# Block products in the mixer's input projections, kept weight sums, paused modulation rows and a reordered start, on an 8-core decoder trunk

## The chip, the cores and the metric

The kernel runs on the eight cores of one Trainium2 chip; each core works on one of eight sequences, with the same weights. The metric is the device time of the slowest core in microseconds (us). Cores 0 to 3 are one die, 4 to 7 the other; I call 0-1, 2-3, 4-5 and 6-7 pairs. Some executions of any kernel fall into a slow state, in which a whole die runs at a lower granted clock; those runs are called slow, and only fast runs are compared unless I say otherwise. The calls for chip time fell on different chips, which are told apart here by their numbers: 8, 14, 4, 10 and 7. The chip of the first measurement is not known.

## The reference, cut to what matters

```python
D_MODEL = 1024; BATCH = 8; SEQ = 2048; DEPTH = 2; D_FF = 2816
# each sub-layer: RMSNorm -> shift/scale from c -> f -> gate -> residual add
# layer 0: SwiGLU, mixer_ab, SwiGLU; layer 1: SwiGLU, mixer_pool, SwiGLU
def mixer_ab(h, w_in, norm_v, w_s, b_s, conv_w, w_out):
    proj = h @ w_in                                # (B, S, 2560)
    u, v, bg, cg, xb = jnp.split(proj, [...], axis=-1)        # 512 columns each
    y_a = spatial_gating(jax.nn.gelu(u), jax.nn.gelu(v), norm_v, w_s, b_s)
    y_b = bg * causal_short_conv(cg * xb, conv_w)
    return jnp.concatenate([y_a, y_b], axis=-1) @ w_out
# mod = silu(c) @ w_mod[l] + b_mod[l]   -> shift, scale and gate of each sub-layer: the "modulation rows"
# ... swiglu, spatial_gating, causal_short_conv, mixer_pool, final RMSNorm
```

The program works in passes of 1,024 tokens, two per sub-layer, each of two tiles of 512 tokens.

## The kernel before

A small list scheduler in the kernel's own code places every instruction on its engine in order of modelled time.

The SwiGLU layers ("FFN" below) already multiply by seven block products in place of eight: a 2 x 2 block matrix product after Strassen and Winograd, with sums of weight blocks and of activation blocks made on DVE, and sums of products made on DVE and ACT. The mixer's input projections u and the three conv sections use plain products:

```python
def u_part(tt, hd):                      # gate u: 8 products per output of 128 x 512
    b = bank(); pc = W["u", hd // 2]; ff = hd % 2
    for c in range(NC):
        mm(PS[b][:], SL[:, pc.slot, (ff * 8 + c) * 128:(ff * 8 + c + 1) * 128], HH.ap(c, tt), c == 0, c == NC - 1, ...)
    act(TP[:, gu, 0:TT], PS[b][:], AF.Gelu_apprx_tanh, ...)
# ... and for the conv sections, three banks at a time:
for si in range(3):
    for c in range(NC):
        mm(PS[b][:], SL[:, pcs[si].slot, ...], HH.ap(c, tt), c == 0, c == NC - 1, ...)
```

Weights lie in six slots in SBUF; a slot is loaded again when its piece has been used up. The modulation rows (144 per core, each a dot product of 131,072 weights with `silu(c)`) are streamed in small portions: sixteen at the start, on which everything waits, and 128 later, one per eight segments of work, wherever the schedule has DVE time:

```python
SLG = (2, 3, 4, 6, 7, 7)     # load of slot s waits for the shift row of chunk SLG[s]
on_pe = (10, 12, 14, 15)     # these four of the first 16 rows are dotted ...
def row0(k):
    for n, q in ((2 * k, c), (2 * k + 1, 8 + c)):
        if n in on_pe:       # ... on PE, by eight products of one column
            for kc in range(NC):
                add("pe", I("matmul", PS[b][:, 0:1], ap[...], CT[:, kc:kc + 1], ...), cost=0.25)
        else:                # DVE: multiply and accumulate, 1.2 us
            stt(ap, ap, 1.0, CB[:], ALU.mult, ALU.mult, ..., accum_out=M)
for s, k in zip(range(NSLOT), SLG):
    load_next(s, [("MOD", 0, order0[k])])
# later rows
def rows_pump():
    row_tick[0] += 1
    if row_tick[0] >= ROW_EVERY and rows_on[0] and slack():
        row_tick[0] -= ROW_EVERY
        # ... take the next row: row_dot(q) on DVE, prefetch another
```

## Time and profile before

| | before |
|---|---|
| median of the first three runs | 1933.72 us (1932.42 to 1934.73) |
| spans of the eight cores in the profiled run | 1921.6 to 1928.1 us |
| PE / DVE / ACT busy | 98% / 88% / 53% |
| f16 products of 512 columns on input projections | 5440 |
| continuous products begin | 67 to 71 us, by core |

A line of the table by stage gives a window, its length, the busy time of each engine with its number of instructions, the granted clock of TensorE as a share of full speed (PEclk), the mean busy share of the 16 DMA engines and their rate. The prediction shows the lines that bound the kernel. One line that it did not look at is the clock row of the page, in tenths of full speed, one digit per fortieth of the span:

```profile
PEclk9899999999999999999999999999999999999999
```

A 9 means 0.9 or more. After the first 100 us the clock is full.

### The profile page before, as it was taken

To read this page: it belongs to the slowest core of one execution; us is meant where nothing else is said; L and a number is where in the kernel's file an instruction comes from. 1 tells how busy PE (TensorE), PEld (TensorE's weight loads), DVE (VectorE), ACT (ScalarE), POOL (GpSimd) and SP (SyncE) were. 2 spreads that over 40 slices of the span, in tenths; PEclk is the share of its full clock that TensorE was granted. 3 is DMA by queue.
4 is the path that set the end of the run, shared out by engine and by line. 5 is a ranking of instruction groups with operands and counts; after the bars stand their busy time and mean duration, and the time that the engine had idled before them with its cause. 6 is when DMAs were issued, how large, how long until landed. Compare 5 with 4: busy or idle time off the path is not lost.

```text
span 1928.1 us, 25440 instructions; the slowest of 8 cores (1921.6 to 1928.1 us)
## 1 busy us (share of the span) xinstructions
PE 1883.1 (98%) x8722; PEld 855.1 (44%) x8722; DVE 1692.6 (88%) x3252; ACT 1030.2 (53%) x1742; POOL 175.9 (9%) x333
## 2 busy tenths in 40 slices
PE   4999999999999999999999999999999999999997
PEld 1544444444444444444444444444444444444443
DVE  4797999999888899999999888888999899998865
ACT  4444854455464564555456554654556655574343
POOL 0000000001112000000000000000000000000000
PEclk9899999999999999999999999999999999999999
DMA  9679658787776676767774554555453545445852
GB/s 277 141 174 220 115 104 188 169 189 152 172 156 153 144 146 160 166 140 151 166 175 80 88 88 85 88 99 87 74 92 66 88 77 97 79 76 85 177 84 92
DMA packets 67661, 248.72 MB, mean 129 GB/s; under 512 B 7632, under 2 KB 7760, under 8 KB 67280
## 3 DMA queue, kind: packets, MB, share of 16 engines
q0 software_dynamic: 42192, 153.64, 47.4%
q1 hardware_dynamic: 25056, 92.67, 15.1%
q8 instruction: 74, 1.21, 0.2%
q10 hardware_dynamic: 288, 0.79, 0.1%
q14 instruction: 51, 0.42, 0.1%
HBM read 392.29 MB, written 8.39 MB: 208 GB/s over the span
## 4 chain that ended last, share of the span: by engine, by line
PE 93%; DMA 4%; SPq 1%; DVE 1%; ACT 0%; issue 0%; POOL 0%
PE ps L480 93%; DMA WMOD<-wmod 3%; SPq L480 1%; DMA SLOTS<-win 1%; DMA ACTB<-wmod 0%; DVE X L480 0%; DVE ACTB L480 0%; DVE WMOD L480 0%; ACT PMH L480 0%; ACT ps L480 0%; ACT ACTB L480 0%; ACT RS L480 0%; ACT L480 0%; DVE TP L480 0%; ACT TP L480 0%
## 5 line engine op out<-in xcount | busy, mean ns | idle before, releaser
L480 PE MATMUL ps<-H,SLOTS 128*128 128x512 f16 x5440 | 1197.4, 379 | 3.1 <-DVE ps L480 1.3
L480 PEld LDWEIGHTS ps<-H,SLOTS 128*128 128x128 f16 x5440 | 531.0, 98 | 648.3 <-issue 14.6
L480 ACT ACTIVATE ps<-ps 128x512 f32<-128x512 f32 x684 | 398.0, 582 | 585.3 <-PE ps L480 577.7
L480 PE MATMUL ps<-ACTB,SLOTS 128*128 128x512 f16 x2780 | 614.2, 379 | 0.8 <-DVE X L480 0.8
L480 PEld LDWEIGHTS ps<-ACTB,SLOTS 128*128 128x128 f16 x2780 | 271.9, 98 | 329.1 <-issue 1.5
L480 DVE TENSOR_TENSOR SLOTS<-SLOTS 128x512 f16<-128x512 f16 x996 | 392.6, 418 | 16.3 <-DMA SLOTS<-win 11.0
L480 DVE SCALAR_TENSOR_TENSOR X<-ps,GH,X 128x512 f32<-128x512 f32 x424 | 307.5, 746 | 34.4 <-PE ps L480 29.4
L480 ACT ACTIVATE TP<-ps 128x512 f32<-128x512 f32 x400 | 237.8, 595 | 124.4 <-PE ps L480 121.9
L480 DVE TENSOR_TENSOR ACTB<-TP,ps 128x512 f16<-128x512 f32 x368 | 248.1, 683 | 33.5 <-PE ps L480 20.9
L480 POOL DMA_DIRECT2D SLOTS<-win x176 | 93.1, 530 | 1039.1 <-PE ps L480 965.3
L480 ACT ACTIVATE SQ<-X 128x512 bf16<-128x512 f32 x224 | 131.0, 622 | 84.2 <-DVE X L480 42.0
L480 DVE TENSOR_TENSOR TP<-ps,TP 128x512 f32<-128x512 f32 x176 | 121.0, 688 | 48.7 <-ACT ps L480 47.6
L480 DVE SCALAR_TENSOR_TENSOR WMOD<-WMOD,CB 128x1024 f32<-128x1024 f32 x130 | 158.0, 1217 | 3.3 <-DMA WMOD<-wmod 3.3
L480 DVE TENSOR_TENSOR ps<-ps,TP 128x512 f32<-128x512 f32 x176 | 122.5, 696 | 13.4 <-PE ps L480 11.4
L480 DVE TENSOR_TENSOR TP<-X,RS 128x512 f32<-128x512 f32 x192 | 127.5, 683 | 6.6 <-ACT ACTB L480 4.8
L480 DVE TENSOR_TENSOR ACTB<-ACTB 128x1024 f16<-128x1024 f16 (+1 forms) x188 | 104.4, 566 | 1.3
L480 POOL DMA_DIRECT2D SLOTS<-wout x88 | 46.5, 528 | 489.4 <-PE ps L480 482.2
L480 PE MATMUL ps<-SQ,ONES 128*128 128x512 bf16 x182 | 59.6, 431 | 28.1 <-ACT SQ L480 25.8
L480 ACT ACTIVATE H<-TP,MODT,AS 128x512 f16<-128x512 f32 x81 | 62.3, 805 | 23.6 <-DVE TP L480 12.0
L480 ACT ACTIVATE PMH<-TP,MODT,AS 128x512 f16<-128x512 f32 x60 | 47.4, 804 | 9.4 <-DVE TP L480 9.3
L480 ACT ACTIVATE ACTB<-TP,MODT,AS 128x512 f16<-128x512 f32 x51 | 40.0, 805 | 13.3 <-PE ps L480 7.1
L480 DVE TENSOR_TENSOR H<-H 128x1024 f16<-128x1024 f16 (+1 forms) x72 | 43.2, 623 | 2.1 <-ACT H L480 2.1
(78 smaller groups left out, 531.5 us busy)
## 6 DMA issues: line engine op xcount, KB each, us to landing
SLOTS<-win POOLq DMA_DIRECT2D x176, 512.0 KB, 5.7
WMOD<-wmod SPq DMA_DIRECT2D x131, 512.0 KB, 5.5
SLOTS<-wout POOLq DMA_DIRECT2D x88, 512.0 KB, 5.4
SLOTS<-wab POOLq DMA_DIRECT2D x28, 512.0 KB, 8.1
outT<-X SPq DMA_DIRECT2D x14, 512.0 KB, 4.5
ACTB<-wmod SPq DMA_DIRECT2D x13, 512.0 KB, 27.9
X<-xT SPq DMA_DIRECT2D x2, 2048.0 KB, 22.0
X<-xT SPq DMA_DIRECT2D x8, 512.0 KB, 9.7
```

The source lines that it names most:

```text
L480: return lambda E: getattr(E, name)(*a, **k)
```

## The change

The intent: seven block products for u and the three conv sections too (64 products fewer in the two passes); the weight block sums of six conv pieces are stored in DRAM by pass one and read by pass two; the normalisation of v moves from DVE to ACT; modulation rows pause in the mixer; and the start is reordered, with one row fewer on PE and the first weight loads later in the queue.

```diff
-SLG = (2, 3, 4, 6, 7, 7)
+SLG = (5, 6, 6, 7, 7, 7)
+AB_KEEP = (4, 5, 6, 7, 8, 9)
@@ sums of the mixer's conv pieces: pass one keeps, pass two reads
+            for n in AB_KEEP:
+                a["w"][AB_PIECES[n]].keep = b["w"][AB_PIECES[n]].kept = n_kept
+                n_kept += 1
@@ rows
-    SLACK = 2.5
+    SLACK = 2
-        rows_on[0] = True
+        rows_on[0] = sub[0] == "F"
+        row_tick[0] = 0
@@ seven products per unit of 256 outputs x 1024 tokens
+    def mix_segments(units):
+        def prod(u, b, wq, hq, first): ...
+        def P1(u): ...
+        # ... P5, P2, P6, P7, P3, P4
+        for w, fs in ((u, (P1, P5)), (v, (P7, P3)), (u, (P2,)), (v, (P4,)), (u, (P6,))): ...
@@ normalisation of v
-            ts(Av4[:, blk, :], TP[:, gv, 0:TT], STAT[:, st, 6:7], STAT[:, st, 9:10], ALU.subtract, ALU.mult, ...)
+            add("pool", I("tensor_scalar", out=STAT[:, st, 10:11], ..., op0=ALU.mult, op1=ALU.mult), ...)
+            act(Av4[:, blk, :], TP[:, gv, 0:TT], AF.Identity, ..., scale=STAT[:, st, 9:10], bias=STAT[:, st, 10:11])
@@ mixer body
-        for tt in range(2):
-            for hd in range(4): u_part(tt, hd) ...
+        for f in mix_segments([u_unit(f) for f in range(2)]): ...
-        for hf in range(2):  # 24 x 8 products
+        for f in mix_segments([mix_unit(sec, hf) for hf in range(2) for sec in (3, 4, 2)]): ...
@@ start
-    on_pe = (10, 12, 14, 15)
+    on_pe = (10, 12, 14)
-                                ..., cost=0.25)
+                                ..., cost=0.43)
```

(The rest of the diff is cut: buffers of the conv chain, the order of pieces, renamed keys.)

## The prediction

> **What bounds the kernel now.** I read the page first, then the chain of waits in order of time, the matmul engine's own waits, a table by stage, the vector engine's groups in the first mixer pass, and the timeline of the start. The page and its chain:
>
> ```profile
> PE 1883.1 (98%) x8722; PEld 855.1 (44%) x8722; DVE 1692.6 (88%) x3252; ACT 1030.2 (53%) x1742; POOL 175.9 (9%) x333
> PE 93%; DMA 4%; SPq 1%; DVE 1%; ACT 0%; issue 0%; POOL 0%
> ```
>
> Busy PE alone proves little, since matmuls are pipelined. What matters is that 93% of the chain is PE following PE, and that PE has almost nothing to wait for after the start; its waits in the whole run, largest first:
>
> ```profile
> PE ps L480 <- ACT SQ L480: 25.8, 3, 18.9
> PE ps L480 <- DVE ps L480: 1.3, 1, 1.3
> PE ps L480 <- DVE X L480: 0.8, 1, 0.8
> ```
>
> The 25.8 us lie in the first 35 us and in the tail. So between about 70 and 1915 us a product removed is a product's time saved, unless another engine takes over. Whether one can is in the table by stage (columns: window and its length, PE, PEld, DVE, ACT, POOL busy with counts, clock, DMA share, GB/s). Rows are the FFN pass before the mixer, the mixer's two passes, the FFN pass after, and two later stretches:
>
> ```profile
> 373.00:474.00 101.00, 101.00 (x469) 45.66 (x468) 98.10 (x190) 58.03 (x97) 9.14 (x17) 1.00 0.80 173
> 474.00:574.00 100.00, 100.00 (x488) 46.30 (x487) 83.76 (x146) 53.98 (x94) 16.02 (x31) 1.00 0.74 168
> 574.00:675.00 101.00, 101.00 (x493) 46.79 (x492) 87.20 (x151) 53.01 (x93) 15.99 (x31) 1.00 0.65 147
> 675.00:775.00 100.00, 100.00 (x465) 45.12 (x463) 96.52 (x195) 50.86 (x87) 8.16 (x16) 1.00 0.71 153
> 1080.00:1180.00 100.00, 100.00 (x465) 45.28 (x463) 79.81 (x152) 50.00 (x86) 8.47 (x17) 1.00 0.51 88
> 1180.00:1280.00 100.00, 99.01 (x459) 44.63 (x458) 89.73 (x173) 57.67 (x97) 8.97 (x17) 1.00 0.54 88
> ```
>
> The reader is to see two things: in the mixer PE is full and DVE has 14 to 16 us spare per pass; and the FFN runs with DVE at 96 to 98% without PE losing a microsecond, so a DVE near 97% is not by itself a stall here. The start is another regime, bound by transfers. Windows of it (same columns), then its timeline:
>
> ```profile
> 42.00:50.00 8.00, 6.60 (x44) 5.04 (x43) 5.92 (x12) 5.80 (x8) 0.53 (x1) 0.93 1.01 235
> 50.00:58.00 8.00, 7.68 (x29) 5.15 (x29) 3.64 (x10) 0.00 (x0) 0.53 (x1) 0.50 1.00 253
> 17.83 0.73 POOL L480 DMA_DIRECT2D SLOTS<-win  x1 [17.15 <-DVE MODT L480]
> 36.68 0.54 POOL L480 DMA_DIRECT2D SLOTS<-win  x1 [18.11 <-DVE MODT L480]
> 42.28 0.53 POOL L480 DMA_DIRECT2D SLOTS<-win  x1 [5.06 <-DVE MODT L480]
> 54.12 3.54 PE L480 MATMUL ps<-CT,WMOD 128*128 128x1 f32 x16 [0.32 <-DMA WMOD<-wmod]
> 57.52 3.55 PE L480 MATMUL ps<-CT,ACTB 128*128 128x1 f32 x16
> 63.88 2.94 PE L480 MATMUL ps<-H,SLOTS 128*128 128x512 f16 x8
> ```
>
> The DMA engines are full, three weight loads were issued in front of the last modulation rows, and the last two rows are then dotted one after the other on PE. Continuous products begin at 70.33 us.
>
> **What the Trainium skill says.** "VectorE: DVE Perf Modes", section on the TRN2 errata, gives a matmul of 512 columns as 518 cycles, 216 ns. "TensorE: Matmul & The Clock Gate", Back-to-back issue gap, gives 131 ns for a stream of them. This trace has 28 products per unit and weight loads 6.05 us apart in steady FFN stretches: 216 ns, the first page's figure. "VectorE: DVE Perf Modes", the perf-mode tier table, gives tensor_tensor the double rate only for 16-bit SBUF operands and the single rate with fp32 or PSUM. The trace agrees: block sums of weights (f16, 512) 418 ns recorded and 392.6/996 = 394 ns busy, adds on PSUM 688 to 697 ns. "DMA: Bandwidth & Descriptors", Issuing engines are not separate DMA queues, says that all issuers share the same 16 engines; the 100% share above with rows from SP and weights from POOL agrees.
>
> **The change part by part.**
>
> *Products removed.* Per pass the gate u had 8 outputs of 8 products (64), the three conv sections 24 x 8 = 192. Now there are 2 + 6 = 8 units of 7 x 4 = 28 products, 224 in place of 256. v and the output projection stay. 32 per pass, 64 in all, x 0.216 us = 13.8 us. A mixer pass goes from 100.2 us (weight release to release, 574.5 to 674.7) to about 93.3.
>
> *DVE in mixer pass one.* From 83.8 us busy: 15 modulation rows leave (the groups show 15 at 1216 ns; with their accumulator reads 18.4); the eight normalising tensor_scalars (537 ns) go to ACT, -4.3. Added: weight sums of 8 units, 32 x 0.394 = 12.6; two adds per unit, 16 x 0.69 = 11.1; activation block sums at double width, 8 x 0.65 = 5.2 (0.65 from 3.9 us for 6 in pass two). Sum: 90.0 of 93.3, that is 96%.
>
> *DVE in pass two.* From 87.2: -17.1 (14 rows), -4.3, + sums of only the two u pieces 3.1 (the six kept ones come from DRAM), + 11.1, + 1.3 for activation sums not already there, + about five rows that must still be done: 6. Sum 87.3 of 94.
>
> *ACT.* 54.0 + three evictions per unit 24 x 0.59 = 14 + norms 8 x 0.8 = 6.4 - 12 staging copies of 0.61 = 67 of 93: not a bound.
>
> *DRAM sums.* Pass one stores six times 0.5 MB; pass two reads 0.5 MB f16 + 0.75 MB f32 in place of 1 MB for six pieces. 4.5 MB more at a mean DMA share of 0.65 to 0.74: hidden, and slots come free once per 6 us unit with several in flight.
>
> *Rows paused.* 29 of the 128 streamed rows (15 + 14) sat in the mixer because unspent ticks piled up in the FFN. Ticks are now reset each pass, so FFN before the mixer gives about 25 (200 segments / 8) in place of 33: 18 + 25 = 43 done, 48 needed for the next norm, hence the five above. The rest, some 24, cross to later FFN passes: 24 x 1.2 = 29 us of DVE. The stretch 1080 to 1280 alone has 30 spare, and all are needed only by about 1250. The busy stretch up to 980 is protected by the smaller slack limit. I count +1 us.
>
> *Start.* One row fewer on PE takes the 3.5 us dot at 57.52 off PE and puts 1.22 us on DVE beside the other. Weight loads now wait for the shift rows of chunks 5, 6, 6, 7, 7, 7 in place of 2, 3, 4, 6, 7, 7. A load costs 47.4% of 1928 us over 292 loads and 16 engines, about 3.1 us of all engines. At least one and perhaps two of the three loads ahead of the last row move behind it: 3 to 6 us. With the dot, up to 6 to 9; against it the first piece and its sums come later, and must land before the first unit. I take 7.
>
> *Stalls in the mixer.* The mean of 96% hides an uneven pass. In u and conv PE has some 12.1 + 1.8 + 36.3 plus a few column-sum matmuls, 51 us. DVE has there z and gating 8 x 1.33 = 10.6, conv and products 8 x (0.65 + 1.45 + 0.65) = 22, unit adds 11, sums of the six b pieces 9.5, squares 2.7: 56. It can run behind into the output projection (27.6 us of PE; DVE 11 updates + 10.5 norm products + 3.9 sums), which is almost full as well. I count 3 us in pass one and 0.5 in pass two.
>
> Sum: 1933.7 - 13.8 + 3.5 + 1 - 7 = 1917.4 us.
>
> **The rivals.** (1) DVE takes over the mixer: each unit's second half waits for its add on DVE, and conv backlog holds PSUM banks. For: the 56 against 51. Against: the FFN lives at 98%, and pass two is lightened. Then 5 to 6 us per pass come back, the mixer gains 2 to 4, and the total is about 1925. (2) The start gains nothing, because the first weights arrive as the rows did and PE waits for SLOTS: about 1924; with rival 1, 1931. (3) The start gains its full transfer share, 10 us or more, since the old order also held PE at half clock (0.50 above) behind the rows: about 1912. (4) The displaced rows crowd the FFN passes, where DVE is at 97%: PE gaps of 1 us as at 894 become several, + 3 to 6 us, about 1921 to 1923.
>
> **Range and chances.** The sure part is 13.8 us, 0.7%. Both uncertain parts, mixer stalls (0 to 11 us back) and the start (0 to 12 gained), are of its size. Eight in ten: 1908 to 1928. Faster by over 2% would need 1895, that is 39 us, nearly double the sure part and the best start together: 2%. Slower by over 2% would need 53 us of new stalls: 1%. Within 2%: 97%.
>
> **What would show it.** Right: 64 fewer f16 products; mixer passes of 93 to 97 us with PE busy throughout; DVE about 96% in pass one and lower in pass two; no row dots there but a handful; the continuous products from 61 to 66 us in place of 70. Wrong step by step: PE waiting for DVE ps or DVE ACTB in the conv stretch (rival 1); PE waiting for DMA SLOTS near 55 us (rival 2) or in pass two (the DRAM sums not hidden); new gaps between 675 and 980 us (rival 4). A median above 1930 would say that DVE, not PE, set the mixer.

## More of the kernel before

An instruction may be filled into a gap that lies earlier in the modelled time of its engine than the point in the program where it was written.

While PE waits at the start it runs filler products on a tile of ones. They are meant to keep its clock up; no run here takes them out, so what they are worth is not shown.

## The result, and the profile after

In the first measurement the changed kernel's fast runs took 1939.81 and 1942.06 us (two more of its four runs were slow), the kernel before 1933.41 us in the median of four. The ratio of fast runs is 1.0038 (95% interval 1.0014 to 1.0063). A ratio is the mean time of one kernel's fast runs over the mean of the other's of the same rounds, so it is not quite the ratio of the medians that I quote. "Within 2%" was foreseen; the time was not: it lies above the range of 1908 to 1928.

The first view to read is the table of cores of the changed kernel (span, mean granted clock):

```profile
core 0: 1938.2 us, clock 0.973
core 1: 1934.4 us, clock 0.979
core 2: 1909.8 us, clock 0.995
...
core 7: 1906.8 us, clock 0.994
```

Six cores lie at 1906.8 to 1911.1 us, some 16 us below those of before. Two lie 27 us above, at a lower clock. The time of a run is that of its slowest core, so the two decide it. The page, which is of core 0, says the same in its clock row:

```profile
PE 1893.0 (98%) x8633; PEld 849.7 (44%) x8633; DVE 1719.3 (89%) x3326; ACT 1056.7 (55%) x1782; POOL 183.0 (9%) x349
PEclk6888899999999999999999999999999999999999
```

Slices two to five are at 0.8, where the kernel before has 0.8 in slice two alone and 0.9 or more from slice three on. All four runs had such cores: in the run at 1942.06 us three pairs took 1936 to 1941 us, and in the two slow runs two or four cores of the die that was not slow took 1935 to 1939. The stage table of the changed kernel's core 0, and below it that of its core 2 (columns as before; the clock is the third from the end):

```profile
60.00:200.00 140.00, 140.00 (x535) 57.87 (x534) 107.18 (x210) 54.47 (x96) 9.50 (x18) 0.81 0.71 152
200.00:240.00 40.00, 40.00 (x170) 17.21 (x169) 35.68 (x70) 29.79 (x48) 3.18 (x6) 0.90 0.64 131
240.00:280.00 40.00, 40.00 (x187) 18.15 (x186) 39.47 (x74) 24.16 (x43) 3.16 (x6) 1.00 0.48 92
```

```profile
60.00:200.00 140.00, 138.52 (x640) 62.25 (x640) 125.76 (x253) 72.86 (x126) 11.61 (x22) 1.00 0.85 181
```

Same program, same 140 us, PE busy throughout on both: 535 products against 640. Core 0 was granted 13/16 of the clock (0.8125). 0.90 over the next 40 us means that the spell ended about 21 us into them. In the clock records behind the view such a spell (there are seven pairs with one in the traces of all runs) lasts 159.5 to 160.5 us, begins 6.6 to 9.2 us after the half-clock time of the start ends, that is, with the first products at full rate, always covers both cores of a pair, and does not return in that run, though products go on just as densely to 1915 us. At 13/16 clock, 160 us of products lose 160 x (1 - 0.8125) = 30 us; the measured cost, pair against the other cores of its run, is 26 to 32 us. No wait and no idle time shows it: PE is busy for 98% of the span, as before.

On the undisturbed cores the rest of the profile can be read against the prediction. The timeline of PE at the start, on core 2 of the changed kernel:

```profile
45.36 3.55 PE L480 MATMUL ps<-CT,WMOD 128*128 128x1 f32 x16 [1.07 <-DMA WMOD<-wmod]
...
55.75 1.89 PE L480 MATMUL ps<-H,SLOTS 128*128 128x512 f16 x8
...
57.91 8.27 PE L480 MATMUL ps<-H,SLOTS 128*128 128x512 f16 x36
```

The last row on PE is done at 49 us in place of 61, and continuous products begin at 57.91 in place of 70.33 on the core that the prediction showed. The first down-projection of this core begins 11.1 us earlier than on the same core before (131.62 against 142.76). Then the two mixer passes on core 2, to be held against the windows 474 to 574 and 574 to 675 of before:

```profile
460.80:557.50 96.70, 93.95 (x452) 42.45 (x453) 87.59 (x164) 64.15 (x111) 18.52 (x39) 1.00 0.71 148
557.50:653.80 96.30, 94.22 (x455) 42.80 (x456) 87.90 (x157) 65.54 (x112) 20.47 (x38) 1.00 0.66 152
```

The windows run from PE's first product of a pass to that of the next; before, these were 99.6 and 100.2 us apart. PE is no longer full: it lacks 2.8 and 2.1 us of busy time. The waits of PE in the mixer, core 2 (engine, tile, what released it: us in total, times, longest), where the kernel before has none at all in its two passes:

```profile
PE ps L480 <- ACT ps L480: 1.6, 3, 0.8
PE ps L480 <- DVE ps L480: 0.9, 3, 0.4
PE ps L480 <- ACT TP L480: 0.8, 1, 0.8
PE ps L480 <- DVE ACTB L480: 0.7, 2, 0.5
```

These are short waits at hand-overs. A sum over the starts of PE's groups, start minus previous start minus count times 0.2158 us (0.0556 us for the products of 128 columns), gives 8.2 us of gaps from 460 to 660 us, against 1.1 us before; it counts also the gaps too short to be listed as waits. On both cores five product records are missing there, which is 1.1 us of each sum; cores with whole records have 7.0 us or more after and 0.04 before. One of the gaps in full, from the timeline of all engines in the first conv stretch:

```profile
515.97 4.48 PE L480 MATMUL ps<-H,SLOTS 128*128 128x512 f16 x20 [0.76 <-ACT ps L480]
...
520.00 0.58 ACT L480 ACTIVATE ps<-ps 128x512 f32<-128x512 f32 x1 [2.47 <-DVE ACTB L480]
...
520.71 2.75 PE L480 MATMUL ps<-H,SLOTS 128*128 128x512 f16 x12 [0.27 <-DVE TP L480]
...
523.23 1.22 DVE L480 SCALAR_TENSOR_TENSOR WMOD<-WMOD,CB 128x1024 f32<-128x1024 f32 x1 [0.80 <-DMA WMOD<-wmod]
...
524.09 4.74 PE L480 MATMUL ps<-H,SLOTS 128*128 128x512 f16 x20 [0.63 <-ACT ps L480]
```

A modulation row (WMOD) stands in the "paused" mixer; DVE first waits 0.80 us for it and then works 1.22 us on it, with the adds of a unit behind it. ACT had waited 2.47 us for DVE, and PE waits for ACT. The list of DVE's groups in the two passes counts the rows:

```profile
L480 DVE SCALAR_TENSOR_TENSOR WMOD<-WMOD,CB 128x1024 f32<-128x1024 f32 x13 | 15.8, 1215 | 0.8 <-DMA WMOD<-wmod 0.8
```

Thirteen, not none: four in pass one and nine in pass two. The switch stops only the rows that are pumped in one per eight segments. Rows that a norm needs are done where the program reaches that norm: the next FFN's norm needs 48 streamed rows, this core had done 37 when the mixer began, so eleven of the thirteen were due by the end of pass two in any case. The program writes them there, and the scheduler filled some into earlier gaps of DVE, four of the rows even in pass one.

### The profile page after: what moved, and what is told of

Same layout as the page of the kernel before. It is cut to its first block, busy times and chain, and to the rows that moved or that the text cites. A ratio compares the mean times of both kernels' runs of the same rounds, so it can differ in the third digit from the quotient of the medians.

```text
span 1938.2 us, 25442 instructions; the slowest of 8 cores (1906.8 to 1938.2 us)
## 1 busy us (share of the span) xinstructions
PE 1893.0 (98%) x8633; PEld 849.7 (44%) x8633; DVE 1719.3 (89%) x3326; ACT 1056.7 (55%) x1782; POOL 183.0 (9%) x349
## 4 chain that ended last, share of the span: by engine, by line
PE 93%; DMA 3%; ACT 2%; DVE 1%; SPq 0%; issue 0%; POOL 0%
PE ps L480 93%; DMA X<-xT 1%; DMA SLOTS<-win 1%; DMA WMOD<-wmod 1%; ACT SQ L480 1%; ACT TP L480 1%; DVE ACTB L480 0%; SPq L480 0%; ACT H L480 0%; ACT ps L480 0%; DVE X L480 0%; DVE TP L480 0%; DVE ps L480 0%; ACT L480 0%; ACT ACTB L480 0%
## 5 line engine op out<-in xcount | busy, mean ns | idle before, releaser
L480 ACT ACTIVATE ps<-ps 128x512 f32<-128x512 f32 x716 | 416.3, 582 | 611.9 <-PE ps L480 601.5
L480 PE MATMUL ps<-ACTB,SLOTS 128*128 128x512 f16 x2780 | 623.1, 382 | 0.0
L480 DVE TENSOR_TENSOR SLOTS<-SLOTS 128x512 f16<-128x512 f16 x1036 | 408.9, 417 | 10.6 <-DMA SLOTS<-win 6.1
L480 DVE TENSOR_TENSOR ACTB<-TP,ps 128x512 f16<-128x512 f32 x352 | 236.8, 682 | 34.4 <-PE ps L480 24.2
L480 DVE TENSOR_TENSOR TP<-ps,TP 128x512 f32<-128x512 f32 x192 | 131.8, 687 | 55.6 <-ACT ps L480 54.4
L480 DVE TENSOR_TENSOR ps<-ps,TP 128x512 f32<-128x512 f32 x192 | 133.4, 695 | 15.6 <-PE ps L480 12.4
L480 ACT ACTIVATE H<-TP,MODT,AS 128x512 f16<-128x512 f32 x105 | 81.2, 806 | 31.9 <-DVE TP L480 31.6
L480 DVE TENSOR_TENSOR H<-H 128x1024 f16<-128x1024 f16 (+1 forms) x88 | 53.9, 634 | 1.7 <-ACT H L480 1.6
L480 ACT ACTIVATE PMH<-TP,MODT,AS 128x512 f16<-128x512 f32 x52 | 41.4, 806 | 11.8 <-DVE TP L480 11.6
L480 PEld LDWEIGHTS ps<-SQ,ONES 128*128 128x128 bf16 x173 | 18.3, 108 | 54.6 <-issue 41.2
```

The lines of the kernel that those rows point to most:

```text
L480: return lambda E: getattr(E, name)(*a, **k)
```

## The experiments

Eleven different kernels were run, some of them again as controls, so eighteen in all, in five calls, each call on one chip with eleven runs of the kernel before beside them. A run counts as "with a spell" when both cores of a pair took 23 to 38 us longer than its undisturbed cores (or, in the one run that has none, than those of other runs of the kernel), at mean clocks of 0.97 to 0.982. Cores that are longer still, at lower clocks, count as slow, and the rest of such a run is still looked at. Only profiled runs have a clock record, so elsewhere a spell is inferred from spans and mean clocks. "Core mean" below is the mean span of the cores without spell or slow state: it measures the work without the clock.

My theory after the first trace: the change does what it should (some 16 us), and the clock spell, set off by the new start, takes it back. The rivals: the spell comes from the denser mixer or from chance, and the gain itself is smaller.

### Call 1, on chip 8: the parts apart

**old_start**, the changed kernel with the old start, so the mixer alone:

```diff
-SLG = (5, 6, 6, 7, 7, 7)
+SLG = (2, 3, 4, 6, 7, 7)
-    on_pe = (10, 12, 14)
+    on_pe = (10, 12, 14, 15)      # and cost 0.43 -> 0.25
```

> The changed kernel with the start of the kernel before (weight loads gated by chunks 2, 3, 4, 6, 7, 7; four rows dotted on PE, costed 0.25). Theory (the new start sets off a spell of 13/16 clock, 160 us long, on some cores): no core at 0.97 to 0.98 clock in any undisturbed run, all cores within 8 us of each other, time about 1927 (1933.4 less the 6.6 us that the mixer gains on undisturbed cores). Rival (the spell comes from the denser program as a whole, not from the start): some cores still at 0.97 to 0.98 and 28 to 31 us longer than others, time about 1950.

Measured: 1924.89 us in the median of six, ratio 0.9947 (0.9934 to 0.9961), four undisturbed runs at 1922.6 to 1926.3; one of six with a spell on pair 2-3 (1955.42). Core mean 1919.8 against 1927.3 before: the mixer alone is worth 7.5 us.

**new_start**, the kernel before with the new start only (the same diff the other way round, on the kernel before):

> The kernel before with only the new start. Theory: undisturbed cores about 11 us shorter than before (1911 to 1917), but in most runs one or more cores with a mean clock of 0.97 to 0.98, 28 to 31 us longer, so a time of 1940 to 1946. Rival: all cores near 1914 at 0.985 or more, and the time is 1917.

Measured: 1920.38 us, ratio 0.9931 (0.9918 to 0.9943). Core mean 1915.5: the start alone is worth 11.8 us. No spell in six runs. This did not fit a theory in which the new start always sets it off.

**old_slots**, the changed kernel with the old order of weight loads but three rows on PE:

```diff
-SLG = (5, 6, 6, 7, 7, 7)
+SLG = (2, 3, 4, 6, 7, 7)
```

> The changed kernel with only the old gates of the first weight loads; three rows on PE stay. If the order of the transfers is what makes the ramp steep, no core at 0.97 to 0.98, start gain reduced to the 3 to 4 us of the one dot, time 1922 to 1925. If the change of the PE rows does it, spells remain and the time is about 1945 to 1950.

Measured: 1924.57 us, ratio 0.9948 (0.9934 to 0.9961), no spell in seven runs. Core mean 1919.1, within 0.7 us of old_start: taking one row off PE is worth next to nothing without the new order of the loads.

**old_pe_rows**, the changed kernel with four rows on PE and the new order of loads:

```diff
-    on_pe = (10, 12, 14)
+    on_pe = (10, 12, 14, 15)      # and cost 0.43 -> 0.25
```

> The changed kernel with only the old rows on PE (four, costed 0.25); late weight loads stay. If late loads make the ramp steep: spells of 13/16 on some cores, undisturbed cores about 1911 to 1914, time about 1940 to 1945. If the PE rows do it: no spell, time 1911 to 1915.

Measured: 1919.69 us in five runs from 1918.90 to 1920.66, ratio 0.9926 (0.9913 to 0.9938), no spell. Core mean 1912.6: the order of the loads carries 7.2 of the start's gain on top of the mixer (1919.8 - 1912.6).

So all four variants beat the kernel before on this chip. What follows for the theory: nothing yet about the trigger, as the changed kernel itself was not among them.

### Call 2, on chip 14: the changed kernel again, and the mixer's stalls

**after_again**, the changed kernel unedited:

> The changed kernel itself once more. Theory (its start, with late weights and three rows on PE together, makes the 13/16 spell likely, since neither half alone and neither mixer did it in 24 runs but once): in at least every second run some core has a mean clock of 0.97 to 0.98, and the fastest run is again near 1940. Rival (the spell is an accident of that chip or hour, which the first four runs met): most runs have every core within 0.985 to 0.998, the time is 1909 to 1915, and the ratio to before is 0.988 to 0.990.

Measured: eight runs; seven with a spell, on one or two pairs of die 1: 1939.0 to 1941.8 us, and two longer ones, 1968.1 (where the second pair of die 1 is 58 to 60 us long, twice a spell) and 1995.7 (where die 0 is longer still); the one without is the fastest, 1913.88. Ratio 0.9968 (0.9906 to 1.0030), from three runs only: a run in which all of die 1 has a spell is marked slow. The kernel before had none in eleven runs.

**old_pe_again**, the same file as old_pe_rows:

> The changed kernel with the old four rows on PE, repeated as the base of the two runs below: 1919 to 1921, no core at 0.97 to 0.98 in the fast runs, if its five clean runs were no accident; if the rival holds, spells may appear here too.

Measured: spells in three of seven runs (1941.06, 1942.52, 1942.88), three undisturbed runs at 1920.2 to 1921.2. On chip 8 the same file had none in five. Ratio 0.9960 (0.9920 to 1.0000). So something that differs from chip to chip, or from call to call, matters (each chip was met in one call only, so the two can't be told apart), and the row on PE is not the cure.

**norm_on_dve**, that kernel with the normalisation of v back on DVE:

```diff
-            add("pool", I("tensor_scalar", out=STAT[:, st, 10:11], ...), ...)
-            act(Av4[:, blk, :], TP[:, gv, 0:TT], AF.Identity, ..., scale=..., bias=...)
+            ts(Av4[:, blk, :], TP[:, gv, 0:TT], STAT[:, st, 6:7], STAT[:, st, 9:10], ALU.subtract, ALU.mult, ...)
```

> Base old_pe_again with the normalisation of v back on DVE, one tensor_scalar in place of a GpSimd product and an ACT pass. If the longer chain over GpSimd and ACT makes PE wait between v and u (about 3 of the 7 us of PE gaps that the trace shows in the mixer lie there), the gaps shrink by 1 to 2 us and the time is 1 to 2 us below the base. If DVE's queue is what fills there, 4.3 us more DVE work per pass make the gaps grow to 9 or more and the time 2 us longer.

Measured: 1944.72 us, ratio 1.0054 (1.0042 to 1.0066), but all five runs had a spell, so the time decides nothing. The traces of undisturbed cores do: gaps on PE from 460 to 660 us sum to 8.9 us on the two cores first read and to no less on any of the eight. In old_pe_again the two cores read had 9.0 and 7.2; the 9.0 is 7.9 without five missing records, and the least of the eight is 7.0. So the gaps grew by some 2 us, and the core mean of the same call, 1914.6 against 1912.5, says the same. Moving the normalisation to ACT did not cause the mixer's stalls; it saved some 2 us of them, as the second branch of the expectation had it.

**rows_out**, old_pe_again with later rows held behind PE's progress after the first FFN, and taken more often there so that they don't run out of time:

```diff
-    ROW_EVERY = 8
+    ROW_EVERY = 6
@@ row_dot, once the mixer has been reached
-        stt(ap, ap, 1.0, CB[:], ALU.mult, ALU.mult, ..., accum_out=MODT[:, q:q + 1])
+        op = add("dve", I("scalar_tensor_tensor", ...), ..., after=Sd.tl["pe"].tail() if seen_mixer[0] else 0.0)
+        if seen_mixer[0]:
+            op.deps.add(last[-1])
```

> Base old_pe_again with the modulation rows truly kept out of the mixer: one every six segments before it and a dependency that keeps later rows from being filled in (3 dots left in place of 12). If rows that leaked into the mixer make the gaps in pass one's conv stretch (3.1 us, where a dot waits for its transfer behind the stores of the sums), gaps fall from 7.1 to about 4 us, time 1916 to 1917. If DVE's conv work alone makes them, they stay at 6 to 7 and the time is unchanged.

Measured: 1944.01 us with spells in four of six runs, one undisturbed run at 1920.90. Ratio 1.0009 (0.9963 to 1.0055). Its trace has three or four rows in the mixer in place of 13 to 15 (cores 0 to 3, 460 to 654 us), and the gaps there fall to 5.7 and 4.5 us on the two cores read. The waits of PE from 455 to 660 us on its core 2:

```profile
PE ps L480 <- ACT ps L480: 1.0, 2, 0.8
PE ps L480 <- DVE ACTB L480: 0.7, 2, 0.5
PE ps L480 <- DVE ps L480: 0.7, 2, 0.4
```

2.4 us in place of 6.3 on the same core of old_pe_again (5.1 on its core 0). So some three of the mixer's seven to nine us of stalls go with the rows. But the undisturbed cores are slower: from 660 to 1160 us the gaps on cores 1 to 3 sum to 5.1 to 7.2 us, where old_pe_again has 0.6 to 0.7, and the core mean is 1915.4 against 1912.5. The rows cost more in the full FFN passes than in the mixer: the prediction's fourth rival, in a kernel that really moves them. (The edit also takes rows more often before the mixer, so it is not the move alone.)

### Call 3, on chip 4: which half of the start goes with the spell

**after_third**, the changed kernel:

> The changed kernel as a control of this chip. On a chip like that of after_again: in most runs one pair of cores (0 and 1, 2 and 3, 4 and 5 or 6 and 7) at 0.97 to 0.98, fast runs near 1940. On a chip like that of the first experiments: none, 1911 to 1914; then the three runs below decide nothing about the spells.

Measured: spells in four of six runs, on pairs 6-7, 0-1 and 2-3, and 0-1 twice; those at 1938.3 to 1941.3 us, the two others at 1913.59 and 1916.95. Ratio 0.9985 (0.9937 to 1.0033).

**new_start_again**, the kernel before with the new start:

> The kernel before with the new start alone. If the start sets off the spells, whatever the mixer: pairs of cores at 0.97 to 0.98 in most runs, time 1945 to 1948. If the new mixer has a part in it: none, 1920.

Measured: spells in two of six runs (1947.99 and 1951.68), undisturbed runs at 1919.25 and 1922.08; in a third, 1984.98, all of die 1 is 44 to 69 us longer, which counts as slow, as in the run of 1995.02 us of old_slots. Ratio 0.9983 (0.9930 to 1.0036). The kernel before had no spell in eleven runs of this call. Its mixer runs here, so the new mixer is not needed for a spell. The rival that put it down to the denser mixer alone falls; whether the new mixer makes spells more frequent, two of six against four of six can't say.

**old_slots_again**, the file of old_slots:

> The changed kernel with only the old gates of the first weight loads, so that the DMA engines fall silent just when the first products run at full clock (share 0.00 to 0.45 between 66 and 74 us in its trace, 0.9 to 1.1 in the changed kernel's first 18 us of products). If full transfers beside the first products set off the spell: none, or at most one in five runs, 1922 to 1925. If an early or steep ramp does, as it does whatever the transfers: spells in most runs, near 1950.

Measured: five fast runs at 1921.34 to 1924.22 without a spell, one in the sixth (pair 4-5 of a run whose other die was slow). Ratio 0.9949 (0.9937 to 0.9961), the same as on chip 8. With the new mixer and the old order of loads the spell came once in six runs, on a chip where the new order (after_third and new_start_again) has it in 6 of 12. Six runs alone don't settle this; the table at the end of this section has more.

What differs when the first full-clock products run? The stage table of one undisturbed core of old_slots_again, in the window from 66 to 74 us:

```profile
66.00:74.00 8.00, 8.00 (x38) 3.52 (x37) 7.38 (x18) 4.92 (x8) 0.53 (x1) 1.00 0.25 39
```

and the same window, with the one before it, of core 6 of after_again, a core with a spell:

```profile
58.00:66.00 8.00, 8.00 (x33) 3.14 (x32) 7.17 (x16) 4.17 (x8) 0.00 (x0) 0.84 1.05 170
66.00:74.00 8.00, 8.00 (x32) 3.29 (x31) 6.72 (x14) 2.92 (x5) 1.06 (x2) 0.81 1.02 220
```

With the old order the DMA engines are a quarter busy when dense products begin; with the new order they are full. And the products begin some 10 us earlier. Either could matter, but neither is enough: core 4 of the same run of after_again, without a spell, has its DMA engines at 1.01 to 1.05 from 58 to 74 us, and its continuous products begin at 55.74 us, those of core 6 at 55.76.

**quiet_ramp**, the changed kernel, with the loads of slots three to five held until PE has begun its first group:

```diff
-    for s, k in zip(range(NSLOT), SLG):
+    for s, k in zip(range(3), SLG):
         load_next(s, [("MOD", 0, order0[k])])
+    # in the first group: after segments 4, 6, 8 of it, load_next(slot 3, 4, 5), each depending on PE's last product
```

> The changed kernel with its early start, but the weight loads of slots 3 to 5 held back until unit 1 runs, some 6 to 9 us after the first product. If full transfers beside the first products set off the spell: no spell, or far fewer than in the control, and 1911 to 1914 in most runs, the best of all versions. If the early ramp by itself does: as many spells as in the control, near 1940.

Measured: spells in two of six runs (1939.67 and 1940.64), four undisturbed at 1916.87 to 1921.47. Ratio 0.9977 (0.9938 to 1.0015). The trace, of an undisturbed run, shows that the transfers were quiet (0.03 to 0.37 of the engines, by core) for 4 us only, from 58 to 62 us. Two of six against four of six is no difference that six runs can show: inconclusive.

### Calls 4 and 5, on chips 10 and 7: transfers against the early start

**noisy_before**, the kernel before with useless copies behind the first weight loads, so that the transfers of the changed kernel stand beside the start of the old one:

```diff
+    for n in range(NOISE):       # NOISE = 6
+        add("pool", I("dma_start", out=spare_d[n], in_=win_d[n]), reads=[("MOD", 0, order0[7])], ...)
```

> The kernel before, unchanged in its products, its start and its weight loads, with six useless copies of 1 MB from DRAM to DRAM queued directly behind the last of the first six weight loads. Before, the DMA engines fall silent from about 66 to 74 us, just when the first steady products begin at full clock; here they should be full from about 60 to 85 us, as in the changed kernel. The kernel before showed no spell at 13/16 clock in any of its 37 runs. If full transfers beside the first products set the spell off: spells of 160 us on a pair of cores in at least two of six runs, those runs near 1960 us (1933 plus 28 to 31, a little less where the pair was not the slowest). If the earlier start of the products itself sets it off: no spell, 1933 to 1938 us (a weight load or two lands later behind the copies).

Measured: 1954.57 us in four runs from 1953.65 to 1955.14, ratio 1.0097 (1.0081 to 1.0113), and no spell. The core mean is 19.7 us above that of the kernel before in this call. Most of it is a wait of PE: 13.1 us on core 3 (10.7 to 13.4 by core) for one weight load that queued behind the copies, and shorter waits after it.

**late_after**, the changed kernel with its first product, in the order of the program, waiting for the sixth weight load:

```diff
+    landed = [("SL", 5, q) for q in range(7)]     # added to the reads of the first product, then cleared
```

> The changed kernel, with its first product waiting until the sixth weight load has landed, so that the products begin at about 76 us, with the transfers quieter, but start just as densely as in the changed kernel. This gives back some 18 us of the start by design: undisturbed cores near 1925 to 1930 us. If full transfers beside the first products set the spell off: spells in none or one of six runs. If the start of dense products after the filler products does, wherever it lies: spells in about half of the runs, those near 1957 us.

Measured: 1933.81 us, ratio 0.9987 (0.9974 to 1.0000), no spell in six runs. Core mean 1924.9, 13.4 above the changed kernel of the same call. But the edit did not do what it was made for. The scheduler placed products written later in front of the one that waits: on core 2 products begin at 56.2 us as in the changed kernel, 32 of them run by 66.6, the waiting ones follow at 69.3, and only from 79.9 are they continuous. All eight cores look like this. So this is an early start with a hole in it, not a late dense start, and the 13.4 us are the cost of the hole.

**after_fourth**, the changed kernel as the control:

> The changed kernel as it is, as the control for this chip: 1913 to 1917 us without a spell, 1938 to 1942 with one; spells in three or more of six runs if this chip is like the last two, in none if it is like the first one. Only in the first case do the other two runs of this call decide anything.

Measured: no spell in five runs; the four fast ones at 1915.94 to 1916.92 us. Ratio 0.9900 (0.9886 to 0.9914). So this chip shows no spell at all, and the call decides nothing on the trigger. But it shows the change without the spell.

**after_fifth**, the control again, on chip 7:

> The changed kernel, as the control for this chip. The chip of the last call showed no spell of 13/16 clock even in the changed kernel (five runs, 1916 to 1917 us without one), so the last call told nothing of the trigger. If this chip shows spells: three or more of six runs at 1938 to 1942 us, the others 1913 to 1917.

Measured: no spell in six runs; the four fast ones at 1912.84 to 1916.98 us. Ratio 0.9899 (0.9861 to 0.9936). The kernel before had one run of eleven with what looks like a spell here (1952.75 us, clock 0.972 on pair 0-1), its only one in 59.

**noisy_before_3**, with three copies in place of six:

> The kernel before with three useless copies of 1 MB directly behind the first six weight loads in place of six. Six cost 20 us by themselves, since later weight loads queued behind the copies and PE waited 13.1 us for one; three should fill the DMA engines from about 60 to 80 us and cost a few us: 1933 to 1945 us without a spell. If full transfers beside the first full-clock products set the spell off, and the control shows spells: pairs of cores with 160 us at 13/16 clock in at least two of six runs, those 20 to 30 us longer. If the earlier start of the products does: none.

Measured: 1946.32 us in the median of six, ratio 1.0054 (1.0008 to 1.0099), fast runs 1942.59 to 1948.60, no spell. Its stage table on core 3 shows that the copies did fill the engines beside the first products (1.09 where old_slots_again has 0.25; shares somewhat above 1 are recorded in other runs too):

```profile
66.00:74.00 8.00, 8.00 (x38) 3.55 (x37) 7.29 (x20) 4.57 (x7) 0.00 (x0) 1.00 1.09 205
```

On a chip where the control has none, that tells nothing.

**late_after_again**, the file of late_after:

> The changed kernel with its first product waiting for the sixth weight load, 1934 us without a spell on the last chip. If the control shows spells here and this doesn't in more than one of six runs, they need the first products at the early time or beside the full transfers; if it shows them in three or more (near 1958 us), the dense start sets them off wherever it lies.

Measured: 1933.51 us in the median of seven, ratio 0.9979 (0.9943 to 1.0015), fast runs from 1925.43 to 1935.52, no spell in seven runs; again without a control that has any, and with the same hole in place of a late start (continuous from 78 to 83 us, by core).

### All spells together

| runs with a spell | chips 14 and 4 | chips 8, 10 and 7 |
|---|---|---|
| the changed kernel | 11 of 14 | 0 of 11 (chips 10 and 7) |
| other kernels with the new order of loads and early products | 16 of 30 | 0 of 11 (chip 8) |
| changed kernel with the old order (old_start, old_slots) | 1 of 6 | 1 of 13 |
| the kernel before | 0 of 22 | 1 of 33 |

The second row adds old_pe_again, norm_on_dve, rows_out, new_start_again and quiet_ramp on the left, new_start and old_pe_rows on the right. In the first measurement all four runs of the changed kernel had one and none of the four of the kernel before. On chips 14 and 4 the new order of the first loads has it in 27 of 44 runs and the old order, with either mixer, in 1 of 28: the new order makes it frequent there, and the old order does not exclude it. What in that order sets it off, transfers beside the first dense products or the earlier start of those products, stays open, as does why three of five chips, or calls, hardly showed it.

A slow run was never traced, but the clocks suggest that the slow state and the spell are kin: in the longest slow runs (2302.11 of old_pe_again, 2307.48 of rows_out) the mean clock of all cores of one die is 0.808 to 0.816, which is what 13/16 (0.8125) over nearly the whole run would give. That is argued from the means, not shown.

Which version is best depends on that. Where no spells occur, it is the changed kernel, at 1916 us. Where they do, old_slots is: 1923.46 us on chip 4, where the changed kernel has 1939.53, and 1924.57 on chip 8, where spells are rare. It beats the kernel before by 0.5% on both.

## Why the prediction was right or wrong

**The sum.** It was 16.3 us off the kernel before, to 1917.4. The core means of cores without a spell fell by 16.4 us (chip 4: 1926.4 to 1910.0), 17.0 (chip 10: 1928.5 to 1911.5) and 15.3 (chip 7: 1926.1 to 1910.8), and the 11 undisturbed runs of the changed kernel lie at 1912.84 to 1916.98, with 1915.94 in the middle. For the work of the engines the total holds. That it does is partly luck, as the terms show.

**The step that failed** is the path that the sum rests on: "So between about 70 and 1915 us a product removed is a product's time saved, unless another engine takes over", with every product at 0.216 us. On the two cores that set the time no other engine took over; the product itself became dearer. On cores 0 and 1, from about 60 to 220 us, the clock was 0.8125, so by these numbers a product took 0.2158 / 0.8125 = 0.266 us, and 160 us of products lost 30 us, against 26 to 32 measured. No step asks what clock the changed start will be granted, and the time is that of the slowest of eight cores, so that one pair of cores sets it. "Range and chances" inherits this: it takes the mixer's stalls and the start as the only uncertain parts. In the first measurement the spell added some 26 us to a kernel that, by the undisturbed runs of the later calls, would have been at 1913 to 1917. What in the new start sets the spell off stays open. A tail on the slow side for a changed start would have been the right form of it; before showed no spell in the runs that I had, so its size could not have been read from them.

**"A median above 1930 would say that DVE, not PE, set the mixer"** was a wrong test. The fast runs were above 1930, and DVE was busy 87.6 of 96.7 us in pass one (91%) where I had worked out 96%. (The working was some 7 us too high: 90.0 us without any row, against 87.6 with four rows of 1.2 us.) A time above the range needed a look at the cores and their clock first.

**Products removed**: right. The group of these products counts 5376 in place of 5440.

**Start**: mis-sized. I took 7 us; continuous products begin some 12 us earlier (core means 69.2 and 56.8), the first down-projection 10 to 11, and the start alone, on the mixer of before, shortens the core mean by 11.8 (chip 8) and 11.3 us (chip 4). My working gave the dot taken off PE 3.5 us and the loads 3 to 6. The runs say nearly all of it is in the order of the loads (7.2 of the mean by old_start against old_pe_rows; the row alone 0.7 by old_start against old_slots). The third rival, 10 us or more, was the true one, and its reason is there too: the half-clock time of the start ends at 62 to 67 us before and at 51 to 55 after, by core.

**Stalls in the mixer**: mis-sized. I took 3 + 0.5; the gaps sum to 7 us more than before. That closes the account of the mixer: 13.8 us of products less 7 of gaps is 6.8, and the two passes shrank from 199.8 to 193.0 us. Two of the signs were named (PE waiting for DVE ps and for DVE ACTB in the conv stretch), but the reason given, DVE near 96%, is not what the trace shows: DVE is at 91% in both passes, and PE waits for ACT as long as for DVE (2.4 and 1.9 us of listed waits), at hand-overs of a chain PE, ACT, DVE, PE in which one long DVE instruction delays the rest. A mean busy share, even a correct one, gave no size for that. (The argument against this rival read 98.10 us of a window of 101 as 98%; it is 97%. And the prediction's list of PE's waits leaves out 2.0, 1.4 and 1.0 us between the lines that it shows; none of them lies in the mixer.) Net, the mixer alone gains 7.5 us of core mean where the terms gave 13.8 - 3.5 - 1 = 9.3.

**Rows paused**: wrong in size. I expected five rows left in the mixer and counted thirteen on core 2 (four and nine). The main error is the count before the mixer: 37 streamed rows done where I had 43, so eleven of the 48 were still due. The smaller one is where they run: I did not think of the scheduler, which may fill a later row into an earlier gap. About three us of the mixer's gaps go with the rows, by rows_out. The fourth rival's sign did not show in the changed kernel: from 660 to 960 us the gaps on cores 3 and 5 sum to 0.1 us, before to 0.7 and 2.2 (cores 0 and 7). New ones of 1.3 us stand at 360 to 460 us and of 1.4 at 1450 to 1750.

**DRAM sums and ACT**: right. PE waits for no weight slot in pass two, the DMA share there is 0.66, and ACT is busy 64 and 66 us where I had 67.

**What does not add up, and what does.** The parts alone give 7.5 + 11.6 = 19.1 us of core mean, the whole 16.2 in the mean of the three chips. In the profiled runs it does add up. The first down-projection begins at 141.0 us before and in old_start at 141.1, in new_start at 130.9, and at 130.5 on the six undisturbed cores of the changed kernel (means of cores): the start is worth 10.1 to 10.5 us. From there to the end it takes 1784.2 us before, 1784.6 in new_start, 1777.7 in old_start and 1778.3 in the changed kernel: the mixer is worth about 6. The parts alone, 10.1 (new_start) and 6.5 (old_start), are 16.6 us, and the whole difference of the spans is 16.4 (1925.2 to 1908.8). The excess of the sum above is in the runs of the kernel before that it is measured against: their core mean is 1927.3 and 1926.4 us in those calls, 1925.2 in the profiled run. What makes them longer is not shown.

## What to carry to other kernels

Look at the table of cores and the row of the clock before any other view: a kernel can be faster on six cores and lose on two, and no wait will show it. A change of the start, when the engines go from waiting to dense work, should be tried on several chips, and a version with a gentler start kept beside it. A switch that pauses work stops it only if the scheduler cannot move it: count the instructions in the trace.

## What the Trainium skill lacked or had wrong

- "TensorE: Matmul & The Clock Gate", section "Seeing it yourself": it describes a limiter that takes a whole die to 13/16 clock within about 5 to 20 us of a third core running dense matmuls, and holds it while the load lasts. The runs show the same 13/16 (0.81) and a start of about this delay (6.6 to 9.2 us after the half-clock time ends), but on a pair of cores, for 159.5 to 160.5 us, and not again in a traced run though all eight cores run dense products to the end; and most cores of most runs at full clock under the same load. The slow state, with mean clocks of a whole die down to 0.81, may be nearer to what the page means; no slow run was traced, so that is not shown.
- The same section has nothing on what differs from chip to chip, or from one call to the next: on two chips 11 of 14 runs of the changed kernel had a spell, on two others 0 of 11.
- The same page, section "Back-to-back issue gap": 131 ns for a product of 512 columns in a stream, and about 216 ns only for an isolated gap; here 216 ns in the stream, as the prediction says.
